# Program order of the input and attention stages bound by edges, and three kinds of small additions placed on GpSimd

## The chip, the cores and the metric

The kernel runs on one core of a Trainium2 chip. Its time is the time of one execution on the device in microseconds (us), and the number that counts is the median of the timed runs. A core has five engines that run side by side, each through its own queue and strictly in that queue's order: TensorE (PE, with its weight loads as PEld), VectorE (DVE), ScalarE (ACT), GpSimd (POOL) and SyncE (SP), which here only issues DMAs. An instruction whose input is not there holds up everything behind it on its engine.

## The reference

One decoder block on a sequence of 1024 tokens with 16 meta tokens ahead, width 1024, in float32. The part that this case turns on is the product with `w_in` (which gives the inputs of a convolution branch, q, k, v and two gates) and stick-breaking attention over 16 heads of 64:

```python
h = xn @ w_in
b_c, c_c, h_c, q, k, v, g_conv, g_attn = jnp.split(h, list(splits), axis=-1)
z = jnp.einsum("bqhd,bkhd->bhqk", qb, kb) * scale
log_beta = jax.nn.log_sigmoid(z)
log_fail = jnp.where(causal, log_beta - z, 0.0)
survive = lax.cumsum(log_fail, axis=3, reverse=True) - log_fail
a = jnp.where(causal, jnp.exp(log_beta + survive), 0.0)
o = jnp.einsum("bhqk,bkhd->bqhd", a, vb)
gate_attn = jax.nn.sigmoid(g_attn + b_gate[1])
merged = gate_conv * branch_conv + gate_attn * branch_attn
```

Behind it come the product with `w_out`, a norm, and a gated MLP with a short convolution. The change does not touch those.

## The kernel before, in words

Products in float32 are made of three matmuls on operands split in a high and a low part: high by high, high by low, low by high. The high part is a copy rounded by ACT, the low part a subtraction (source minus high) on DVE or POOL.

**Stages.** From 0 to about 560 us the input stage multiplies by `w_in` (partly in Strassen form) and writes q, k and v to DRAM as `qh_d`, `ql_d`, `kh_d`, `kl_d`, `vv_d`. From 560 to about 990 us runs attention. Behind it come the projections, the merge and the MLP, to 2028 us.

**Attention.** The work is cut in 8 pairs of heads, 2 heads each (`h`), 3 groups of query blocks each (`g`): 48 units. A group has three blocks of 114 queries. For each block:

- `scores` (lines 965 and 966): PE makes `z` of up to 512 keys at a time; it needs `qh`, `ql` and `kk`, which SP loads from DRAM for each head (`load_h`, six DMAs, lines 939 to 941) and `vv` once for a pair (`load_v`, lines 925 and 926).
- `fails` (line 971): ACT turns `z` into `fl` by a sigmoid.
- `scan` (line 982): one DVE instruction over all keys of the block, 128 to 1040 columns, in place in `fl`. It runs along the keys, so no part of `fl` is ready before the scan ends.

Then for each block of keys of the unit:

- `turn` (line 1001): PE transposes `fl` into `tp`.
- `high` and `lower` (lines 1006 and 447): ACT copies `tp` into `ah`, and DVE makes `al` = `tp` - `ah`. DVE alone does this.
- `weigh` (lines 1016 and 1017): PE adds `vv` by `ah`, then `vv` by `al`, to `av`.

A unit ends with three small steps: ACT copies one half of `av` into `half` (line 1039) and the other into `ot` (line 1042), and `out3` adds `half` to `ot` (line 1046). After the sixth unit of a pair `last_add` adds the column `ends` (line 1059), and SP stores `ot` (line 1062).

**Gates.** PE fills its time with the products of the gates: `plain` loads the raw weights of a gate (line 358), ACT makes `whi` (line 457), and two pieces of 512 columns make `wlo` (`lo_piece`, line 369). Then come 24 steps of three matmuls (lines 345 to 347), a sigmoid on ACT for each third (line 670), and a store of the gate (line 673). The first gate after the input stage is the bridge gate, still in the input stage; the twelve mid gates are made within attention. The weights of the first mid gate are prepared in the input stage already, so the first raw weights that attention loads are those of the second and third mid gate.

**What sets the order.** Each stage puts its steps into a `Plan`: engine, cost, key (a due time) and what has to be done before. `run` goes through a simulated time and always starts the ready step with the lowest key on each engine; the step's instructions are emitted at that moment. A step on `"ANY"` goes to whichever of DVE and POOL is free first in this simulation, and a `port` shared by POOL's work and the scans keeps the two apart in it. The emitted order is not the end of it: the framework has a scheduler of its own, which may put the instructions of an engine in another order as long as data dependences hold. `in_program_order` (at the end of the file) is meant to forbid this: it gives every instruction an edge to the one emitted before it on the same engine, over the range of instructions that two numbers mark. The range is taken from `first`, set ahead of the input stage's plan (line 440), and `last`, set behind attention's (line 1075). But `last` is assigned again in the last stage of the kernel (line 1671, `last = gi == len(groups) - 1`), so that the call at line 1718 gets `True`, and the range from `first` to 1 is empty: no edge is made.

Of the kernel before, what the change touches and what calls it, by code (L numbers as in the profile page):

```python
# [11 lines left out]
F32 = mybir.dt.float32  # L12
# [5 lines left out]
P = 128  # L18
# [5 lines left out]
NQ = NT - T0  # L24
CH = NQ // 3
# [89 lines left out]
def pe_cost(n):  # L115
    return (n / 2.4 + 13.0) / 1000.0


def act_cost(n):
    return 0.045 + 0.00091 * n  # L120


def dve_cost(n):
    return 0.07 + 0.00104 * n


def pool_cost(n):
    return 0.06 + 0.0023 * n


def any_cost(n):
    return {"DVE": dve_cost(n), "POOL": pool_cost(n)}
# [3 lines left out]
def block_kernel(ctx, tc, x, meta_tokens, g_pre_mix, w_in, channels, w_proj_conv,  # L136
                 w_proj_attn, w_out, g_post_mix, g_pre_ffn, w_up_gate, w_down,
                 g_post_ffn, out):
    nc = tc.nc

    def pool(name, bufs=1, side="left", space=None):
        kw = dict(name=name, bufs=bufs, reuse_waits="tile")
        if space is not None:
            kw["space"] = space
        else:
            kw["side"] = side
        return tc.tile_pool(**kw)
# [194 lines left out]
    def plain_step(ps, hi, lo, kb, a, n):  # L342
        k = slice(kb * P, (kb + 1) * P)
        xh, xl = src_x(kb, a, n)
        nc.tensor.matmul(ps, hi[:, k], xh, start=(kb == 0), stop=False)
        nc.tensor.matmul(ps, hi[:, k], xl, start=False, stop=False)
        nc.tensor.matmul(ps, lo[:, k], xh, start=False, stop=(kb == KB - 1))
# [8 lines left out]
    def load_raw(o):  # L356
        raw = wpool.tile([P, D], F32, name="raw", tag="raw")
        nc.sync.dma_start(raw, w_in[o])
        return raw

    def whole(raw):
        hi = wpool.tile([P, D], F32R, name="whi", tag="whi")
        lo = wpool.tile([P, D], F32R, name="wlo", tag="wlo")
        return hi, lo

    def lo_piece(raw, hi, lo, i, e="POOL", width=256):
        c = slice(width * i, width * i + width)
        eng = nc.vector if e == "DVE" else nc.gpsimd
        eng.tensor_tensor(lo[:, c], raw[:, c], hi[:, c].bitcast(F32), op=ALU.subtract)

    with ExitStack() as p0:
# [38 lines left out]
        for c in range(3):  # L410
            for b in range(3):
                x_block(3 * c + b)
                if c > 0 and b < 2:
                    if c == 1:
                        raw = first_raw[b]
                        hi, lo = whole(raw)
# [20 lines left out]
    tmp_e = sring.tile([P, 512], F32, name="tmp_e")  # L437
    snap_t = sring.tile([P, 2, 3, HS], F32, name="snap_e")

    first = len(nc.cur_bb.bb.instructions)  # L440
    plan = Plan({"raw": 2, "whi": 0, "wlo": 0, "ap": 4, "wk": 5, "st": 8, "xw": 2})

    def engine_of(e):
        return nc.vector if e == "DVE" else nc.gpsimd
# [1 line left out]
    def low(eng, out, src, hi):  # L446
        eng.tensor_tensor(out, src, hi.bitcast(F32), op=ALU.subtract)  # L447

    def plain(o, chunks, key, make, evac, finish, psum, first_chunk=0, given=None):
        st = {}  # L450
        if given is None:
            def load():
                st["raw"] = load_raw(o)

            def high():
                st["hi"], st["lo"] = whole(st["raw"])
                nc.scalar.copy(st["hi"], st["raw"])

            ld = plan.add("SP", 0.4, load, key=key - 16, takes=("raw",))
            h = plan.add("ACT", act_cost(D), high, (ld,), key - 10, ("whi", "wlo"))  # L460
            los = [plan.add("ANY", any_cost(512),
                            lambda e, i=i: lo_piece(st["raw"], st["hi"], st["lo"], i, e, 512), (h,),
                            key - 9 + 3 * i) for i in range(2)]
            plan.join(los, ("raw",))
        else:
            st["hi"], st["lo"], los = given
        before, evacs = None, []
        for ci in range(first_chunk, 3):
            a, n = chunks[ci]

            def step(kb, ci=ci, a=a, n=n):
                if kb == 0:
                    st["ps", ci] = psum()[:, :n]
                plain_step(st["ps", ci], st["hi"], st["lo"], kb, a, n)

            for kb in range(KB):
                at = key + (8 * (ci - first_chunk) + kb) * 3 * pe_cost(CH)
                before = plan.add("PE", 3 * pe_cost(n), lambda kb=kb, step=step: step(kb),
                                  (before, los[kb // 4] if los else None), at,
                                  (plan_bank,) if kb == 0 else ())  # L480

            def out(ci=ci, a=a, n=n):
                if ci == first_chunk and make is not None:
                    make()
                evac(a, n, st["ps", ci])

            evacs.append(plan.add("ACT", act_cost(n), out, (before,) + tuple(evacs[-1:]), at - 4,
                                  ("wk",) if ci == first_chunk and first_chunk == 0 else (),
                                  (plan_bank,)))
        plan.join((before,), ("whi", "wlo"))  # L490
        finish(evacs[-1:], at)
# [125 lines left out]
    for kb in range(4):  # L617
        st = {}
# [15 lines left out]
        key, t_step = 14.0 * kb, 3.0  # L634
# [3 lines left out]
        for j, (name, dst, x1, x2) in enumerate((("T1", "o1", "o1", "e1"), ("T2", "o1", "o2", "o1"),  # L638
# [12 lines left out]
            h = plan.add("ACT", act_cost(HT), high, (d,), k2)  # L651
# [8 lines left out]
    def late_tile(u):  # L660
        return lambda: u["t"]
# [37 lines left out]
    for i, name in enumerate((("v", 0), ("q", 0))):  # L699
        u = {"t": first_out[i]}  # L700
        o, k, done = block[name]
        plain(o, CH_K, at, None, lambda a, n, ps, u=u: nc.scalar.copy(u["t"][:, a:a + n], ps),
              lambda after, key, done=done, k=k, u=u: done(k, late_tile(u), after, key), bank,
              2, (*first_ops[i], None))
        at += item / 3
    for name in (("k", 0), ("v", 1), ("q", 1), ("k", 1)):
        o, k, done = block[name]
# [23 lines left out]
    def strassen_pair(i, at):  # L731
# [49 lines left out]
        evacs = [[], []]  # L781
        made = [None, None]
        b = {}
        last = {}

        def product(k, s, which, start, tok, hold):
            name = names[k]
# [44 lines left out]
        p = {}  # L832
# [43 lines left out]
    def next_high():  # L876
# [4 lines left out]
    h = plan.add("ACT", act_cost(D), next_high, (ld,), at - 10, ("whi", "wlo"))  # L881
# [9 lines left out]
    ps_mm = psA.enter_context(pool("ps_mm", 2, space=PSUM))  # L891
# [13 lines left out]
    plan = Plan({"raw": 2, "whi": 1, "wlo": 1, "mm": 2, "z": 2, "tp": 3, "av": 1, "qk": 3, "vv": 2,  # L905
                 "ot": 2, "wk": 2, "ah": 4, "al": 4, "half": 1, **{f"fl{b}": n for b, n in enumerate(FL)}})
# [12 lines left out]
    for p in range(NPAIR):  # L919
        ot_parts = []  # L920
# [9 lines left out]
        for h in range(2):  # L930
# [18 lines left out]
            for g in range(3):  # L949
# [38 lines left out]
                ust, readers, last_av = {}, {b: [] for b in scans}, av_last  # L988
# [44 lines left out]
                a0, b0 = (0, 64) if h == 0 else (64, 0)  # L1033
# [7 lines left out]
                def out2(g=g, p=p, a0=a0, ust=ust):  # L1041
                    nc.scalar.copy(out_tiles[p][a0:a0 + 64, CH * g:CH * (g + 1)], ust["av"][a0:a0 + 64])

                def out3(e, g=g, p=p, a0=a0, ust=ust):
                    o = out_tiles[p][a0:a0 + 64, CH * g:CH * (g + 1)]
                    engine_of(e).tensor_tensor(o, o, ust["half"][a0:a0 + 64], op=ALU.add)

                t_o = t_av + share[g] * half_pair
                o1 = plan.add("ACT", act_cost(CH), out1, (last_av,), t_o - 4,
                              ("half", "ot") if (h, g) == (0, 0) else ("half",))  # L1050
                o2 = plan.add("ACT", act_cost(CH), out2, (last_av, o1), t_o - 4, (), ())
                plan.join((o1, o2), ("av",))
                ot_parts.append(plan.add("ANY", any_cost(CH), out3, (o1, o2), t_o, (), ("half",)))
            plan.join(z_users, ("qk",))
        plan.join(v_users, ("vv",))

        def last_add(e, p=p):
            ov = out_tiles[p][:, :NQ].rearrange("p (b n) -> p b n", n=QB)
            engine_of(e).tensor_tensor(ov, ov, ends[:, p].unsqueeze(2).to_broadcast([P, 9, QB]), op=ALU.add)

        fin = plan.add("ANY", any_cost(NQ), last_add, tuple(ot_parts), t_o + 1)
        plan.add("SP", 0.4, lambda p=p: nc.sync.dma_start(o_d[p * P:(p + 1) * P, :], out_tiles[p][:, :NQ]),
                 (fin,), t_o + 1, (), ("ot",))

    for i, (which, ob) in enumerate(mid_gates):
        key = whole_time * i / len(mid_gates)
        outs = gate_out(which, ob, lambda: work.tile([P, NT], F32, name="gt", tag="wk", bufs=2), ("wk",))
        if i == 0:
            plain(0, CH_Q, key, *outs, lambda: ps_mm.tile([P, 512], F32, name="mm", tag="mm"), 0,
                  (nxt["hi"], nxt["lo"], None))  # L1070
        else:
            plain(48 + 8 * which + ob, CH_Q, key, *outs,
                  lambda: ps_mm.tile([P, 512], F32, name="mm", tag="mm"))
    plan.run()
    last = len(nc.cur_bb.bb.instructions)
    psA.close()

    work_ctx.close()
# [532 lines left out]
    for i in range(1, len(pairs)):  # L1611
        p, gate = divmod(i, 2)
# [57 lines left out]
    for gi, fbs in enumerate(groups):  # L1670
        last = gi == len(groups) - 1
# [13 lines left out]
        for tb in range(8):  # L1685
# [3 lines left out]
            for hf in range(2):  # L1689
# [13 lines left out]
                if last:  # L1703
                    sq = dw.tile([P, 512], F32, name="sq", tag="sq", bufs=2)
                    nc.scalar.activation(sq, a, AF.Square, accum_out=ssqs[tb][:, hf:hf + 1])
                    eng = nc.vector if (tb == 7 and hf) else nc.gpsimd
                    eng.tensor_tensor(a, a, g_post2[:, c], op=ALU.mult)
            next(prep, None)
            if last:
# [3 lines left out]
                for hf in range(2):  # L1713
# [1 line left out]
                    nc.vector.scalar_tensor_tensor(a[:, c], a[:, c], r, hb[:, c],  # L1715
                                                   op0=ALU.mult, op1=ALU.add)
                    (nc.sync if hf else nc.scalar).dma_start(out[tb * P:(tb + 1) * P, c], a[:, c])
    in_program_order(tc, nc, first, last)


def in_program_order(tc, nc, first, last):
    before = {}
    for ins in list(nc.cur_bb.bb.instructions)[first:last]:
        if ins.engine in before:
            tc.add_manual_dep(ins, before[ins.engine].name,
                              mybir.DependencyInfo(mybir.DependencyClass.NoSync,
                                                   mybir.DependencyReason.DATA),
                              reason="program order")
        before[ins.engine] = ins
# [57 lines left out]
```

## Time and profile before

| | us |
|---|---|
| median of 3 runs | 2033.87 |
| lowest and highest run | 2029.52 and 2034.86 |
| the profiled execution | 2030.09 |
| its span, first to last instruction | 2028.3 |

The page of the profiled execution gives these busy times over the whole span (share of it, instructions):

```profile
PE 1931.6 (95%) x12732; PEld 1811.0 (89%) x12732; DVE 1161.1 (57%) x1784; ACT 842.6 (42%) x1766; POOL 580.1 (29%) x432
```

Such a row is a mean over stages that differ. In a row of a stretch, further down, the numbers are start and end, length, then the busy us of PE, PEld, DVE, ACT and POOL with the number of instructions in brackets, the clock granted to TensorE (1.00 is full speed), the busy share of the DMA engines, and GB/s. In a row of a wait, the engine with its tile and line stands ahead of the arrow, and what it waited for behind it; then total us, how often, and the longest. In a row of the timeline the first two numbers are start and duration, and square brackets hold the idle time ahead of the instruction and what ended it.

### The profile page before, as it was taken

What the parts mean: (1) busy time and instruction counts of PE and PEld (TensorE: products, weight loads), DVE (VectorE), ACT (ScalarE), POOL (GpSimd) and SP (SyncE); (2) the same over time, 40 slices, a digit from 0 to 9 for tenths busy, and PEclk for the clock granted to TensorE, in tenths of its full rate; (3) what the DMA queues carried; (4) which work ended last, traced back from release to release, by engine and by line L of the source; (5) the groups of instructions that cost most, each with busy time, mean ns of one, the idle gap of its engine ahead of it and who ended that gap; (6) DMA issues with size and microseconds to landing.
All of it is one profiled execution on the core that took longest, in us unless ns stands there. A gap on an engine that the chain in (4) does not pass through costs nothing.

```text
span 2028.3 us, 32023 instructions
## 1 busy us (share of the span) xinstructions
PE 1931.6 (95%) x12732; PEld 1811.0 (89%) x12732; DVE 1161.1 (57%) x1784; ACT 842.6 (42%) x1766; POOL 580.1 (29%) x432
## 2 busy tenths in 40 slices
PE   6999999999988998989999999979999999999997
PEld 6999999999988888888899999968988998878886
DVE  6846666656368778787641116884354435345547
ACT  5533333444355566565541223453344344321122
POOL 1110000001101010010122560336555555654353
PEclk9999999999989999999999999989999999999999
DMA  3522222455684445441285673313221212253223
GB/s 137 161 84 74 83 64 64 145 143 166 181 187 127 118 128 128 113 117 58 84 271 148 188 211 124 105 32 118 70 84 63 104 63 84 75 182 117 84 84 135
DMA packets 73842, 238.56 MB, mean 118 GB/s; under 512 B 15400, under 2 KB 17224, under 8 KB 72668
## 3 DMA queue, kind: packets, MB, share of 16 engines
q1 hardware_dynamic: 70368, 226.00, 37.4%
q10 hardware_dynamic: 3324, 10.50, 1.6%
q8 instruction: 100, 1.64, 0.3%
q14 instruction: 50, 0.41, 0.1%
HBM read 166.02 MB, written 70.46 MB: 117 GB/s over the span
## 4 chain that ended last, share of the span: by engine, by line
PE 74%; DVE 13%; DMA 5%; ACT 3%; POOL 2%; issue 2%; SPq 0%; ACTq 0%; DVEq 0%; POOLq 0%
PE st L796 7%; PE st L799 7%; PE st L798 7%; PE st L1403 6%; PE st L1407 6%; PE st L1405 6%; DVE fl L982 5%; PE st L1697 3%; PE st L1695 3%; PE st L1696 3%; PE mm L245 2%; PE tp L1001 2%; PE mm L246 2%; PE mm L247 2%; DVE al L447 2%
## 5 line engine op out<-in xcount | busy, mean ns | idle before, releaser
L982 DVE TENSOR_TENSOR_SCAN fl<-fl,upper 114x128 f32<-114x128 f32 (+3 forms) x144 | 205.6, 1445 | 30.8 <-ACT fl L971 18.9
L173 POOL TENSOR_TENSOR a_op<-raw,a_op 128x512 fp32r<-128x512 f32 (+1 forms) x136 | 192.5, 1428 | 87.7 <-ACT a_op L172 85.5
L796 PE MATMUL st<-tT,s_op 128*128 128x260 f32 x672 | 190.9, 284 | 0.0
L799 PE MATMUL st<-tT,s_op 128*128 128x260 f32 x672 | 190.1, 283 | 0.0
L798 PE MATMUL st<-tT,s_op 128*128 128x260 f32 x672 | 190.0, 283 | 0.0
L1403 PE MATMUL st<-opT,a_op 128*128 128x258 f32 (+2 forms) x528 | 171.0, 324 | 5.2 <-ACT snap L1418 3.1
L1405 PE MATMUL st<-opT,a_op 128*128 128x258 f32 (+2 forms) x528 | 168.9, 320 | 2.6 <-DVE opT L173 1.7
L1407 PE MATMUL st<-opT,a_op 128*128 128x258 f32 (+2 forms) x528 | 168.7, 320 | 0.0
L1702 DVE TENSOR_TENSOR acc<-acc,st 128x512 f32<-128x512 f32 x144 | 98.4, 687 | 91.2 <-PE st L1697 91.2
L172 ACT CAST a_op<-raw 128x512 fp32r<-128x512 f32 (+1 forms) x136 | 85.1, 634 | 155.9 <-DMA raw<-in_w_up_gate_dram 52.7
L1006 ACT CAST ah<-tp 114x342 fp32r<-114x342 f32 (+3 forms) x288 | 105.8, 403 | 95.3 <-PE tp L1001 91.2
L447 DVE TENSOR_TENSOR al<-tp,ah 114x342 fp32r<-114x342 f32 (+3 forms) x288 | 118.0, 442 | 45.7 <-ACT ah L1006 44.1
L796 PE MATMUL st<-xnT,s_op 128*128 128x260 f32 x504 | 142.4, 283 | 0.0
L799 PE MATMUL st<-xnT,s_op 128*128 128x260 f32 x504 | 142.3, 282 | 0.0
L798 PE MATMUL st<-xnT,s_op 128*128 128x260 f32 x504 | 141.8, 281 | 0.0
L176 DVE TENSOR_TENSOR raw<-raw 128x512 f32<-128x512 f32 x72 | 73.8, 1026 | 108.1 <-POOL a_op L173 106.3
L751 ACT CAST s_op<-raw 128x512 fp32r<-128x512 f32 x126 | 78.2, 622 | 135.4 <-PE st L799 115.5
L447 DVE TENSOR_TENSOR s_op<-raw,s_op 128x512 fp32r<-128x512 f32 x121 | 84.4, 698 | 78.8 <-ACT s_op L751 78.3
L1017 PE MATMUL av<-al,vv 114*128 114x342 f32 (+3 forms) x288 | 92.1, 332 | 38.3 <-DVE al L447 37.5
L1405 PE MATMUL st<-opB,a_op 128*128 128x512 f32 (+2 forms) x396 | 127.4, 322 | 0.0
L1403 PE MATMUL st<-opB,a_op 128*128 128x512 f32 (+2 forms) x396 | 127.4, 322 | 0.0
L1407 PE MATMUL st<-opB,a_op 128*128 128x512 f32 (+2 forms) x396 | 126.9, 321 | 0.0
(224 smaller groups left out, 5880.4 us busy)
## 6 DMA issues: line engine op xcount, KB each, us to landing
raw<-in_w_in_dram SPq DMA_DIRECT2D x64, 512.0 KB
raw<-in_w_up_gate_dram SPq DMA_DIRECT2D x44, 512.0 KB
act_d<-owork SPq DMA_DIRECT2D x22, 512.0 KB
araw<-act_d SPq DMA_DIRECT2D x22, 512.0 KB
raw<-in_w_down_dram SPq DMA_DIRECT2D x22, 512.0 KB
qh<-qh_d SPq DMA_DIRECT2D x32, 256.5 KB
ql<-ql_d SPq DMA_DIRECT2D x32, 256.5 KB
vv_d<-vt SPq DMA_DIRECT2D x16, 512.0 KB
```

Source lines behind the costliest of these rows:

```text
L173: (lo_engine or nc.vector).tensor_tensor(lo, src, hi.bitcast(F32), op=ALU.subtract)
L447: eng.tensor_tensor(out, src, hi.bitcast(F32), op=ALU.subtract)
L796: nc.tensor.matmul(ps, wt[:, 0, c], xh, start=start and kb == 0, stop=False, skip_group_check=True)
L798: nc.tensor.matmul(ps, wt[:, 0, c], xl, start=False, stop=False, skip_group_check=True)
L799: nc.tensor.matmul(ps, wt[:, 1, c], xh, start=False, stop=kb == 3, skip_group_check=True)
L982: nc.vector.tensor_tensor_scan(fl[:, ::-1], fl[:, ::-1], upper[:, NT - nk:][:, ::-1], 1.0, op0=ALU.mult, op1=ALU.max)
L1006: nc.scalar.copy(kst["ah"][:n, off:], kst["tp"][:n, off:CH])
L1017: nc.tensor.matmul(av[:, off:], w, kst["al"][:n, off:], start=False, stop=(kb == nkb - 1))
L1403: nc.tensor.matmul(ps, wt[:, 0, k], xh, start=start and kb == 0, stop=False, skip_group_check=True)
L1405: nc.tensor.matmul(ps, wt[:, 0, k], xl, start=False, stop=False, skip_group_check=True)
L1407: nc.tensor.matmul(ps, wt[:, 1, k], xh, start=False, stop=stop and kb == 3, skip_group_check=True)
L1702: nc.vector.tensor_tensor(a, a, ps, op=ALU.add)
```

## The change

It has two parts.

First, the two marks get names of their own, `pin_from` and `pin_to`, which nothing assigns again. So the edges are made: in the input stage, in attention and in what lies between, every engine's instructions, SP's DMAs included, keep the order in which the plans emitted them.

Second, three kinds of steps of attention's plan go from `"ANY"` to `"POOL"`, with POOL's cost: `out3` (48 additions of 64x342), `last_add` (8 of 128x1026), and the `wlo` pieces of the mid gates that attention's plan itself prepares (11 gates, two pieces each of 128x512). The gates and products of the input stage keep `"ANY"`.

```diff
-    first = len(nc.cur_bb.bb.instructions)
+    pin_from = len(nc.cur_bb.bb.instructions)
...
-    def plain(o, chunks, key, make, evac, finish, psum, first_chunk=0, given=None):
+    def plain(o, chunks, key, make, evac, finish, psum, first_chunk=0, given=None, eng="ANY"):
...
-            los = [plan.add("ANY", any_cost(512),
-                            lambda e, i=i: lo_piece(st["raw"], st["hi"], st["lo"], i, e, 512), (h,),
+            los = [plan.add(eng, any_cost(512) if eng == "ANY" else pool_cost(512),
+                            lambda e="POOL", i=i: lo_piece(st["raw"], st["hi"], st["lo"], i, e, 512), (h,),
                             key - 9 + 3 * i) for i in range(2)]
...
-        last = {}
...
-                def out3(e, g=g, p=p, a0=a0, ust=ust):
+                def out3(e="POOL", g=g, p=p, a0=a0, ust=ust):
...
-                ot_parts.append(plan.add("ANY", any_cost(CH), out3, (o1, o2), t_o, (), ("half",)))
+                ot_parts.append(plan.add("POOL", pool_cost(CH), out3, (o1, o2), t_o, (), ("half",)))
...
-        def last_add(e, p=p):
+        def last_add(e="POOL", p=p):
...
-        fin = plan.add("ANY", any_cost(NQ), last_add, tuple(ot_parts), t_o + 1)
+        fin = plan.add("POOL", pool_cost(NQ), last_add, tuple(ot_parts), t_o + 1)
...
             plain(48 + 8 * which + ob, CH_Q, key, *outs,
-                  lambda: ps_mm.tile([P, 512], F32, name="mm", tag="mm"))
+                  lambda: ps_mm.tile([P, 512], F32, name="mm", tag="mm"), eng="POOL")
     plan.run()
-    last = len(nc.cur_bb.bb.instructions)
+    pin_to = len(nc.cur_bb.bb.instructions)
...
-    in_program_order(tc, nc, first, last)
+    in_program_order(tc, nc, pin_from, pin_to)
```

The names of lines behind 784 are one less after the change, since the line `last = {}` is gone (it was not used there).

What this does to the queues shows in the order of instructions. On DVE, in the unit that runs at 624 to 632 us before, these rows stood one after the other (L982 is a scan, named for its opcode; L447 makes `al`; L1046 is `out3`):

```order
L982 SCALAR_TENSOR_TENSOR fl_6960<-fl_6960,upper_6120 114x812
L1046 TENSOR_TENSOR ot_6385<-ot_6385,half_6981 64x342
L447 TENSOR_TENSOR al_7008<-tp_6977,ah_6993 128x342
L447 TENSOR_TENSOR al_7015<-tp_6986,ah_6998 114x228
L982 SCALAR_TENSOR_TENSOR fl_7006<-fl_7006,upper_6120 114x926
L447 TENSOR_TENSOR al_7024<-tp_7001,ah_7020 114x114
L447 TENSOR_TENSOR al_7044<-tp_7026,ah_7036 128x342
L1046 TENSOR_TENSOR ot_7041<-ot_7041,half_7042 64x342
L447 TENSOR_TENSOR al_7093<-tp_7032,ah_7056 114x342
L447 TENSOR_TENSOR al_7124<-tp_7051,ah_7070 114x342
```

At the same place on DVE after the change (numbers of buffers shift a little, L981 is the scan):

```order
L981 SCALAR_TENSOR_TENSOR fl_6963<-fl_6963,upper_6120 114x812
L447 TENSOR_TENSOR al_7006<-tp_6980,ah_6996 128x342
L447 TENSOR_TENSOR al_7013<-tp_6989,ah_7001 114x228
L447 TENSOR_TENSOR al_7027<-tp_7004,ah_7023 114x114
L447 TENSOR_TENSOR al_7047<-tp_7029,ah_7039 128x342
L981 SCALAR_TENSOR_TENSOR fl_7011<-fl_7011,upper_6120 114x926
L447 TENSOR_TENSOR al_7092<-tp_7035,ah_7058 114x342
L447 TENSOR_TENSOR al_7101<-tp_7053,ah_7073 114x342
```

The scan of 926 columns goes behind the `al` of 114x114 that ends the unit and behind the first `al` of the next one, and the two `ot` additions are gone to POOL.

On SP, at the change from the input stage to attention, the last stores of k, q and v and the first loads of heads stood so before (L358 is a raw weight of a mid gate, here the second's and the third's; L597 stores v, L552 and L554 store q and k; L939 begins the loads of the first head):

```order
L358 DMA raw<-in_w_in_dram 128x1024
L597 DMA vv_d<-vt 128x1024 x2
L597 DMA vv_d<-vt 114x256
L358 DMA raw<-in_w_in_dram 128x1024
L552 DMA qh_d<-hi 128x1026
L554 DMA ql_d<-su 128x1026
L552 DMA kh_d<-hi 128x1040
L554 DMA kl_d<-su 128x1040
L939 DMA qh<-qh_d 64x1026
```

After the change the stores of k are followed by the store of the bridge gate (L673), which stood five loads further back, and then by the loads of heads and of `vv` without a break:

```order
L554 DMA kl_d<-su 128x1040
L673 DMA ga_d<-gt 128x1026
L938 DMA qh<-qh_d 64x1026
L939 DMA kk<-kh_d 64x1040
L940 DMA ql<-ql_d 64x1026
```

The same queue of SP after the change, 18 loads of heads and one pair of `vv` loads further on:

```order
L939 DMA kk<-kl_d 64x1040
L940 DMA ql<-ql_d 64x1026
L924 DMA vv<-vv_d 128x2048
L925 DMA vv<-vv_d 114x256
L358 DMA raw<-in_w_in_dram 128x1024 x2
L673 DMA ga_d<-gt 128x1026
```

The two raw weights have moved from ahead of all loads of heads to behind those of three heads and of both `vv`. On ACT the cast of the first of them (L457) moved likewise, from ahead of the bridge gate's last sigmoid to behind the eight sigmoids of attention's first scores.

## The prediction

> **What bounds the kernel now.** I read the busy time by stretch first, with the granted clock beside it. Columns: stretch and its length, busy us (instructions) of PE, PEld, DVE, ACT and POOL, clock, DMA share, GB/s.
>
> ```profile
> 44.00:558.00 514.00, 513.95 (x4124) 513.55 (x4122) 308.96 (x469) 208.51 (x420) 46.21 (x36) 1.00 0.39 115
> 560.00:990.00 430.00, 384.95 (x2553) 358.78 (x2554) 333.43 (x469) 257.97 (x657) 47.76 (x32) 0.97 0.46 118
> ```
>
> The first row is the input stage, the second attention; the edges cover both. In the input stage PE is busy 513.95 of 514 us at full clock: an order that serves PE better has nothing to win there. In attention PE stands idle 430 - 384.95 = 45 us, and a clock of 0.97 costs 0.03 x 430 = 13 us more. Everything the change can win is in these 58 us. The view of waits over 550 to 1010 us says what PE waited for (total, times, longest).
>
> ```profile
> DVE al L447 <- ACT ah L1006: 44.1, 42, 2.7
> PE av L1017 <- DVE al L447: 37.5, 32, 2.6
> DVE ot L1046 <- ACT ot L1042: 25.2, 23, 2.6
> PE z L966 <- DMA ql<-ql_d: 4.1, 1, 4.1
> ACT half L1039 <- POOL ot L1046: 3.9, 3, 1.3
> ```
>
> 37.5 us of the 45 are one wait: the second matmul of a weigh step (`av`, line 1017) waits for DVE's `al`; another 4.1 are the first scores waiting for a load. No row has PE waiting for a scan. DVE is busy only 333 of 430 us, so it does not lack time; what stands ahead of the awaited `al` in DVE's queue decides. The timeline at 626 to 631 us, rows of DVE, POOL and PE (start, duration), and the clock around it:
>
> ```profile
> 626.42 0.51 DVE L1046 TENSOR_TENSOR ot<-ot,half 64x342 f32<-64x342 f32 x1
> 627.08 1.91 POOL L1059 TENSOR_TENSOR ot<-ot,ends 128x1026 f32<-128x1026 f32 x1 [19.67 <-DVE ot L1046]
> 627.70 3.23 DVE L982 TENSOR_TENSOR_SCAN fl<-fl,upper 114x926 f32<-114x926 f32 x1
> 630.85 0.67 DVE L447 TENSOR_TENSOR al<-tp,ah 114x114 fp32r<-114x114 f32 x2
> 631.15 0.32 PE L1017 MATMUL av<-al,vv 114*128 114x114 f32 x1 [2.58 <-DVE al L447]
> ...
> 628.55:631.15 2.60, 0.02 (x2) 0.00 (x1) 2.60 (x3) 0.43 (x1) 0.43 (x1) 1.00 0.82 324
> 631.97:635.38 3.41, 3.41 (x15) 3.33 (x14) 1.45 (x3) 1.86 (x6) 0.00 (x0) 0.50 0.00 0
> ```
>
> A scan of 926 columns stands ahead of a small `al`; PE idles 2.58 us for it and then runs 3.41 us at half clock, which costs 1.7 us more. The same shape comes back every pair of heads; the last long one is this.
>
> ```profile
> 959.49 0.34 PE L1017 MATMUL av<-al,vv 114*128 114x114 f32 x1 [2.51 <-DVE al L447]
> ```
>
> On the clock, the Trainium skill ("TensorE: Matmul & The Clock Gate", on why this matters for your kernels) puts the bound for a drop at idle gaps of about 3 us. By that rule gaps of this size would cost nothing beyond themselves and the win below would be about 6 us smaller. The rows above differ, 2.58 us was enough, and the measurement decides.
>
> **The change, part by part.**
>
> *Edges, attention, DVE.* In the order shown with the change, the scan of 926 goes behind the two `al` that it held up, and the `ot` addition leaves the queue. I followed the 32 waits of the `al` row in the same way: nearly all have, ahead of the `al`, a scan that goes behind the `al`, or an `ot` addition that leaves DVE. So what can be had is 37.5 us of gaps and, of the 13 us of clock, the part behind these gaps, some 9: 46 us. Not all of it comes. An `al` that no scan holds still needs ACT's `ah` (44.1 us of DVE waits in the list). I take 70%: **-32 us**; the bounds are 30% (-14) and 90% (-41).
>
> What is late next is the scan: put behind up to a few `al` of 0.50 us each (the row of groups below), it ends later for the transposes that read it. Before, PE never waited for one. The longest, 1040 columns, occurs 16 times; one `al` too many on each is 16 x 0.50 = 8 us, none is 0. I take **+4 us**, the middle, since neither end is nearer to a row.
>
> *Additions and low parts on GpSimd.* Groups of attention by form (times | busy us, mean ns):
>
> ```profile
> L1046 POOL TENSOR_TENSOR ot<-ot,half 64x342 f32<-64x342 f32 x4 | 7.0, 1738 | 37.6 <-ACT ot L1042 37.6
> L1046 DVE TENSOR_TENSOR ot<-ot,half 64x342 f32<-64x342 f32 x44 | 23.3, 531 | 25.6 <-ACT ot L1042 25.2
> L1059 DVE TENSOR_TENSOR ot<-ot,ends 128x1026 f32<-128x1026 f32 x4 | 4.9, 1221 | 0.0
> L447 DVE TENSOR_TENSOR al<-tp,ah 114x342 fp32r<-114x342 f32 x144 | 69.2, 501 | 30.0 <-ACT ah L1006 29.4
> L982 DVE TENSOR_TENSOR_SCAN fl<-fl,upper 114x926 f32<-114x926 f32 x16 | 37.6, 2352 | 2.5 <-ACT fl L971 2.5
> L982 DVE TENSOR_TENSOR_SCAN fl<-fl,upper 114x1040 f32<-114x1040 f32 x16 | 37.1, 2318 | 3.6 <-ACT fl L971 3.6
> ...
> 591.32 0.83 POOL L1046 TENSOR_TENSOR ot<-ot,half 64x342 f32<-64x342 f32 x1 [16.24 <-ACT ot L1042]
> ```
>
> DVE loses 23.3 + 4.9 = 28 us of work and the 25.2 us that it stood blocked behind ACT in front of an `ot` (part of what cures the gaps, so not counted again). POOL gains 44 additions of 0.83 (alone, last row) to 1.74 us (mean beside DVE's work) and four of 1.9: 44 to 84 us on an engine that is busy 48 of 430. That it is slower than DVE there shows on PE only through `half`, whose next writer is ACT: the 3.9 us row is that wait with only four additions on POOL. A unit of heads lasts about 9 us (430/48), so an addition of 1.7 us is done long before. Cost nothing there, at most 4.
>
> The price is on the scans. The 926 scans take 2352 ns, more than the 1040 ones at 2318; by width 926 is worth 2064, so those that lie beside POOL's work pay. The Trainium skill ("SBUF — State Buffer", on who interferes with whom) has the rule that an instruction of DVE with two SBUF inputs and one of GpSimd lock each other out, while an operand in PSUM leaves DVE free. It speaks against the change; the 3.23 us scan agrees with it, and `al`, which reads PSUM, keeps its 501 ns. From the rows: scans fill about half of attention, so half of 44 to 84 us, 22 to 42, can come back onto DVE against 28 taken off. DVE's busy time ends between -6 and +14. It has 97 us of slack, so I count 0, with +10 as the bad end.
>
> *Edges, first loads of attention (SP).* This is the loss. Before, SP issues the raw weights of the second and third mid gate at 528.53 and 534.95, ahead of all loads of heads. With the edges the same two stand behind the 18 loads of three half pairs and two of `vv` (order shown with the change). The timeline and DMA rows:
>
> ```profile
> 528.53 0.33 SPq L358 DMA_DIRECT2D raw<-in_w_in_dram  x1
> 534.95 0.34 SPq L358 DMA_DIRECT2D raw<-in_w_in_dram  x1
> 553.36 0.33 SPq L673 DMA_DIRECT2D ga_d<-gt  x1
> 562.38 0.45 PE L966 MATMUL z<-kk,ql 128*114 128x128 f32 x1 [4.14 <-DMA ql<-ql_d]
> 572.14 1.06 ACT L457 CAST whi<-raw 128x1024 fp32r<-128x1024 f32 x1 [0.76 <-issue]
> 573.32 0.41 PE L345 MATMUL mm<-xnT,whi 128*128 128x342 f32 x1
> ...
> ql<-ql_d SPq DMA_DIRECT2D x8, 256.5 KB
> kk<-kl_d SPq DMA_DIRECT2D x4, 260.0 KB
> vv<-vv_d SPq DMA_DIRECT2D x2, 1024.0 KB
> ga_d<-gt SPq DMA_DIRECT2D x2, 513.0 KB
> raw<-in_w_in_dram SPq DMA_DIRECT2D x2, 512.0 KB
> ...
> 552.50:587.50 35.00, 29.09 (x167) 27.68 (x166) 20.68 (x25) 15.23 (x37) 1.80 (x1) 0.86 1.04 226
> ```
>
> The store of the gate (line 673) now heads this row of loads; it waits for ACT's sigmoid, which comes about 1 us earlier since the cast of the raw weights no longer lies ahead of it: start at about 552.5. Ahead of and with the first raw then go 0.53 (store) + 18 x 0.264 + 2 x 1.05 and small remainders + 0.52 = about 8.1 MB. At 226 GB/s, the rate of this stretch with all DMA engines full (share 1.04), that is 36 us: it lands at 588.5. Then ACT's cast 1.06, POOL's first low part (1.80, the one piece in this row), and PE can go on at about 591, where it took up the second mid gate at 573.32 before. PE's order there is unchanged, and it is served strictly in order: nothing behind can step in. **+18 us.** ACT is stuck in its queue on the same cast, with the casts `ah` of the first unit behind a second such cast, so that the first `av` is late again by 1 to 2 us: +1.5. After so long a gap the clock falls; the longest such stretch in the trace is
>
> ```profile
> 1324.88:1335.12 10.24, 4.96 (x24) 4.99 (x25) 7.33 (x14) 6.62 (x9) 0.00 (x0) 0.50 0.16 49
> ```
>
> and costs half of its 4.96 us of PE work: +2.5. Together **+22 us**. Bounds: +13 (the loads served faster, no second delay) and +29 (twice the clock loss, the raw 4 us later).
>
> *Input stage.* ACT, DVE and SP change places a little while PE is full: 0, at most +2 if a load slips behind stores. *End of attention.* POOL instead of DVE for the last addition and the `ends`: 1.7 + 1.9 against 0.53 + 1.22, +1 us, of which gates hide most: +0.5. Everything after 990 us is the same.
>
> **Sum:** -32 + 4 + 0 + 22 + 0.5 = -5.5 us. The profiled execution took 2030.09 us (span 2028.3 of it): 2024.6. The three timed runs lie from 2029.52 to 2034.86 about 2033.87, so the profiled one is a fast one among them; I say **2025 us** for the median.
>
> **The rivals.**
>
> *Slower: lock-out of the scans.* Place: every unit's `ot` addition falls beside a scan, on the way to the `al` that PE waits for. Price: such a scan ends 1.2 us later, as the 926 did at 627.70 (3.23 against 2.06), and PE with it. Five hits (6 us) bring the sum above before, ten above it by more than a measurement can miss; 15 of the 48 additions give back 18 of the 32 us. Time: 2030 - 14 + 4 + 22 = **2042**. For it: the 926 row and the 3.23 us. Against: after the change few scans stand right ahead of an awaited `al`. Chance 0.25. The Trainium skill's rule on who interferes with whom would lead here, if it ruled in every third unit.
>
> *No change: the gain is paid back at the first gate.* The steady part wins about 22, as PE then waits for `ah` through `al`, and the late weights cost 22: **2031** with the small terms. For it: 44.1 us of `al` waiting for ACT. Chance 0.28.
>
> *Full gain.* The raw weights land by about 580 (a shorter queue than I add up) and nine tenths of the gaps go: 2030 - 41 + 8 = **1997**. Against: the DMA share of 1.04. Chance 0.09.
>
> *The edges bind nothing.* Then only the GpSimd part is left. The rows of SP and DVE do change places, so I give it nothing.
>
> **How the numbers follow.** The forecast has 0.38, with its own range of 2012 to 2029. A difference under 0.3% (6 us) cannot be told from none by measuring this kernel. Below 2028: the forecast nearly whole (0.36) and full gain (0.09), with a little of the rival at 2031 (0.02): 0.47. Above 2040: the lock-out nearly whole, 0.23, and 0.03 for a first gate at its bad end: 0.26. Between: 0.27. For 8 in 10, I leave out the better part of full gain and the worst of the lock-out: 2002 to 2047.
>
> **What would show each step.** The wait PE `av` <- DVE `al` should fall from 37.5 to about 12, with a new row of `tp` <- `fl` of some 4 us, and the clock in the steady part to rise to 0.99. DVE's row `ot` vanishes; POOL has 48 of 0.83 to 1.8 us. The mean of the scans of 926 shows the lock-out: above 2.6 us it rules. In the stretch 565 to 600 a single PE gap of about 18 us should wait for `whi` or `wlo`, behind a raw landing near 588. If that gap is under 8 us, the sum falls to near 2010; if `av` <- `al` stays above 25 us, the time is 2035 or more.

## The result and the profile after

| | before | after |
|---|---|---|
| median of 4 runs, us | 2034.22 | 2004.04 |
| lowest and highest | 2029.52 and 2034.86 | 1999.84 and 2005.19 |
| the profiled execution, us | 2030.09 | 2005.19 |

The ratio is 0.9853, with a 95% interval of 0.9832 to 0.9874. The kernel is 30 us faster by these medians, 24.9 by the two profiled executions. Runs of the kernel before beside the later experiments have medians of 2027 to 2031, so that 23 to 30 us is what can be said. The direction was forecast; the gain is about three times the 9 us that 2025 stood for.

To see where it comes from, I compared the end of each head's last `av` (the second matmul of `weigh`) in the two traces. PE has done the same number of matmuls by then in both (4501 at the end of the first head, later within 9), so that the times can be set against each other. After is ahead by 0.75 us in the input stage, behind by 16.2 us at the end of the first head, ahead by 28.7 at the end of attention, and by 25.0 at the end of the kernel. So attention first loses 17 us, then gains 45, and 4 are lost behind it.

**The loss.** The timeline of after at the start of attention (start, duration):

```profile
574.51 0.75 PE L1000 MATMUL tp<-ident,fl 114*128 114x114 f32 x6
576.48 1.63 SPq L358 DMA_DIRECT2D raw<-in_w_in_dram  x2
588.01 1.04 ACT L457 CAST whi<-raw 128x1024 fp32r<-128x1024 f32 x1 [14.96 <-DMA raw<-in_w_in_dram]
589.14 3.75 POOL L369 TENSOR_TENSOR wlo<-raw,whi 128x512 fp32r<-128x512 f32 x3 [47.90 <-ACT whi L457]
590.90 0.73 PE L964 MATMUL z<-kk,qh 128*114 128x464 f32 x1 [15.64 <-ACT fl L970]
```

This is the stall that was forecast: the raw weights were there at 588.0 (forecast 588.5), and PE went on at 590.9 (forecast 591). The gap is 15.6 us and not 18, since PE had work up to 575.3 where the forecast has it stop at 573.3. It is put down to a sigmoid `fl` and not to `whi`: these scores stand just ahead of the gate's product in PE's order, and their sigmoid stood on ACT behind the casts.

**The gain.** Waits of after, the first two from 590 to 970 us, the others from 550 to 990:

```profile
PE z L964 <- ACT fl L970: 16.5, 2, 15.6
PE av L1016 <- DVE al L447: 7.1, 12, 1.4
...
DVE al L447 <- ACT ah L1005: 77.6, 64, 16.9
PE z L964 <- DMA kk<-kl_d: 5.1, 1, 5.1
PEld tp L1000 <- DVE fl L981: 1.0, 3, 0.3
```

PE's wait for `al` fell from 37.5 to 7.1 us. DVE's own wait for ACT's `ah` rose from 44.1 to 77.6 (16.9 of it in the stall), and outside of the stall PE does not feel it. No scan makes PE's weight loads wait more than 0.3 us. From the end of the first head to the end of attention, before and then after:

```profile
599.30:998.62 399.32, 358.29 (x2398) 332.25 (x2397) 312.48 (x447) 242.10 (x617) 45.14 (x30) 0.98 0.40 106
615.54:969.91 354.37, 345.30 (x2398) 326.61 (x2398) 285.87 (x399) 238.00 (x617) 104.85 (x78) 1.00 0.44 119
```

For the same 2398 matmuls PE's idle time falls from 41 to 9 us, which makes 32 of the 45 us. The other 13 are busy time. The clock, 0.98 before and 1.00 after, accounts for about 8 of them (0.02 x 399); the remaining 5 are not explained. A stretch in the middle of attention, before (two pairs of heads) and then after (slightly more, two pairs take 96.8 us there):

```profile
729.70:839.40 109.70, 98.27 (x662) 91.87 (x661) 85.69 (x122) 65.85 (x168) 11.80 (x7) 0.98 0.46 119
```

```profile
715.00:813.00 98.00, 96.22 (x670) 91.58 (x670) 79.53 (x109) 65.02 (x169) 27.96 (x20) 1.00 0.50 133
560.00:970.00 410.00, 381.94 (x2614) 362.24 (x2615) 311.14 (x432) 259.31 (x670) 111.55 (x84) 0.97 0.48 127
```

PE idled 11.4 us of 109.7 and now 1.8 of 98, at full clock. The clock of the whole of attention still stands at 0.97 (second row), and that is the stall's doing: behind the first head it is 1.00, as shown above.

**DVE and GpSimd.** Groups of before:

```profile
L982 DVE TENSOR_TENSOR_SCAN fl<-fl,upper 114x128 f32<-114x128 f32 (+3 forms) x144 | 205.6, 1445 | 30.8 <-ACT fl L971 18.9
```

The same groups of after, then two forms of scans and POOL's additions:

```profile
L981 DVE TENSOR_TENSOR_SCAN fl<-fl,upper 114x470 f32<-114x470 f32 (+3 forms) x144 | 207.8, 1461 | 37.3 <-ACT fl L970 36.7
...
L981 DVE TENSOR_TENSOR_SCAN fl<-fl,upper 114x1040 f32<-114x1040 f32 x16 | 42.9, 2681 | 0.6 <-ACT fl L970 0.6
L981 DVE TENSOR_TENSOR_SCAN fl<-fl,upper 114x926 f32<-114x926 f32 x16 | 33.9, 2118 | 1.9 <-ACT fl L970 1.9
L1045 POOL TENSOR_TENSOR ot<-ot,half 64x342 f32<-64x342 f32 x48 | 59.8, 1246 | 211.1 <-ACT ot L1041 211.0
L1058 POOL TENSOR_TENSOR ot<-ot,ends 128x1026 f32<-128x1026 f32 x8 | 15.2, 1904 | 0.6
```

POOL's busy time in attention rises from 48 to 112 us, and all 144 scans together take 2.2 us more. That is not the price of POOL's work alone, since the scans stand in another order too; the section on e8 separates the two. Which scans are slow has changed: the 926 went from 2352 to 2118 ns, the 1040 from 2318 to 2681.

### The profile page after: what moved, and what is told of

The parts are those of the page before. It is cut to its first block, busy times and chain, and to the rows that moved or that the text cites. A ratio compares the mean times of both kernels' runs of the same rounds, so it can differ in the third digit from the quotient of the medians.

```text
span 2003.3 us, 32045 instructions
## 1 busy us (share of the span) xinstructions
PE 1922.9 (96%) x12732; PEld 1809.7 (90%) x12732; DVE 1129.5 (56%) x1730; ACT 838.2 (42%) x1766; POOL 646.9 (32%) x486
## 4 chain that ended last, share of the span: by engine, by line
PE 76%; DVE 10%; DMA 6%; ACT 3%; POOL 3%; issue 2%; SPq 0%; ACTq 0%; DVEq 0%; POOLq 0%
PE st L798 7%; PE st L795 7%; PE st L797 7%; PE st L1402 6%; PE st L1406 5%; PE st L1404 5%; DVE fl L981 3%; PE st L1696 3%; PE st L1694 3%; PE st L1695 3%; PE tp L1000 2%; PE mm L245 2%; PE mm L246 2%; PE mm L247 2%; PE mm L345 2%
## 5 line engine op out<-in xcount | busy, mean ns | idle before, releaser
L981 DVE TENSOR_TENSOR_SCAN fl<-fl,upper 114x470 f32<-114x470 f32 (+3 forms) x144 | 207.8, 1461 | 37.3 <-ACT fl L970 36.7
L447 DVE TENSOR_TENSOR al<-tp,ah 114x342 fp32r<-114x342 f32 (+3 forms) x288 | 116.4, 441 | 78.5 <-ACT ah L1005 77.6
L1045 POOL TENSOR_TENSOR ot<-ot,half 64x342 f32<-64x342 f32 x48 | 59.8, 1246 | 211.1 <-ACT ot L1041 211.0
L798 PEld LDWEIGHTS st<-tT,s_op 128*128 128x128 f32 x672 | 126.8, 189 | 0.0
```

Source lines behind the costliest of these rows:

```text
L798: nc.tensor.matmul(ps, wt[:, 1, c], xh, start=False, stop=kb == 3, skip_group_check=True)
L981: nc.vector.tensor_tensor_scan(fl[:, ::-1], fl[:, ::-1], upper[:, NT - nk:][:, ::-1], 1.0, op0=ALU.mult, op1=ALU.max)
```

## The experiments

My theory (A): the edges make the steady gain through DVE's order, SP's order costs some 17 to 22 us at the first gate, and the move to GpSimd does next to nothing. Times are medians; a ratio is to the kernel before beside them. In each fence of waits the columns are total us, times, longest.

| run | bound by edges | us | ratio (95% interval) |
|---|---|---|---|
| e1 | all, additions free | 2003.66 | 0.9877 (0.9851 to 0.9904) |
| e2 | none, additions on GpSimd | 2032.27 | 1.0011 (0.9996 to 1.0026) |
| e3 | all but SP | 1980.87 | 0.9764 (0.9739 to 0.9790) |
| e4 | all, weights due earlier | 1986.43 | 0.9794 (0.9767 to 0.9822) |
| e5 | DVE alone | 1985.45 | 0.9790 (0.9766 to 0.9815) |
| e6 | PE, ACT and POOL | 2037.10 | 1.0042 (1.0026 to 1.0058) |
| e7 | all but SP, scans due earlier | 1980.65 | 0.9771 (0.9749 to 0.9793) |
| e8 | all but SP, additions free | 1982.79 | 0.9775 (0.9753 to 0.9798) |
| e9 | all but SP, scans put ahead on DVE | 2033.93 | 1.0023 (1.0009 to 1.0036) |
| e10 | SP alone | 2044.59 | 1.0067 (1.0048 to 1.0086) |

### e1 and e2: one part each

e1 is the kernel before with the two marks renamed:

```diff
-    in_program_order(tc, nc, first, last)
+    in_program_order(tc, nc, pin_from, pin_to)
```

> Only the edges, the three kinds of additions stay free to go to DVE or GpSimd. Theory A (DVE's order makes the steady gain of 45 us, the change of SP's order costs 17 us at the first gate): 2004 to 2012 us, and PE's wait for al in the steady part falls to between 7 and 20 us. Rival B (taking the additions off DVE makes the steady gain): the loss at the first gate stays and little is gained, 2035 to 2050 us, the wait for al stays near 35 us.

e2 is the changed kernel without that call:

```diff
-    in_program_order(tc, nc, pin_from, pin_to)
```

> Only the additions and low parts on GpSimd, no edges. Theory A: 2022 to 2036 us, the wait for al stays above 25 us since the scans still stand ahead of it. Rival B: 1985 to 1995 us, the steady gain without the late weights.

The waits of PE in e1, at the first gate and for `al`:

```profile
PE mm L345 <- ACT whi L457: 13.9, 1, 13.9
PE av L1017 <- DVE al L447: 7.4, 12, 1.1
```

The wait of PE in e2:

```profile
PE av L1016 <- DVE al L447: 41.7, 36, 3.0
```

The edges alone give the whole result, stall and gain, and here PE's gap waits for `whi`. GpSimd alone gives no change: its interval takes in 1. Rival B falls. In the one trace of e2 this is the sum of two parts: e2 is 9.0 us ahead of before at the end of the first head and 0.8 at the end of attention.

### e3 and e4: the late weights

In e3 the loop that makes the edges passes over SP, so that SP's queue at the first gate is again that of before while all other engines keep the order of after:

```diff
     for ins in list(nc.cur_bb.bb.instructions)[first:last]:
+        if ins.engine == mybir.EngineType.SP:
+            continue
```

> The changed kernel with the edges on every engine but SP; SP then stands in the order of before, all other engines in that of after. Theory A: the PE gap of 15.6 us at the first gate goes, and with it 15 to 19 us of the time: 1985 to 1990 us. Rival C (the steady part takes up the lost time anyway, since the loads that come late there were early for the later heads): 1998 to 2005 us.

e4 keeps all edges and gives the loads of the first two raw weights a due time of their own:

```diff
-            ld = plan.add("SP", 0.4, load, key=key - 16, takes=("raw",))
+            ld = plan.add("SP", 0.4, load, key=key - 16 if due is None else due, takes=("raw",))
...
+                  due=-30.0 if i < 3 else None)
```

> The changed kernel with all edges; the two raw weights get a due time that puts them behind the first head's loads and the first vv, ahead of the second head's. Theory A: the first raw lands at about 572, ahead of its use at 575, and the time is 1986 to 1992 us. Rival C: 1998 to 2005 us. If the second head's loads, now 1 MB later, are what PE waits for next, a gap waiting for qh, kk or ql shows and the time is 1992 to 1998 us.

PE's waits in e3:

```profile
PE av L1016 <- DVE al L447: 8.1, 13, 1.4
PE z L965 <- DMA ql<-ql_d: 2.9, 1, 2.9
```

PE's waits in e4, and ACT's wait for the raw weights there:

```profile
PE av L1016 <- DVE al L447: 7.8, 12, 1.4
PE z L964 <- DMA kk<-kl_d: 5.1, 1, 5.1
...
568.83 1.04 ACT L457 CAST whi<-raw 128x1024 fp32r<-128x1024 f32 x1 [2.85 <-DMA raw<-in_w_in_dram]
```

The stall goes in both. e3 is 2004.04 - 1980.87 = 23 us faster than the change. In the two traces the instructions of PE, DVE, ACT and POOL stand in the same order throughout, and SP's differ in one stretch of 32 DMAs, where attention begins: 23 us is the price of SP's order there. Rival C, that the steady part takes it up, falls: after is 21.7 us behind e3 at the end of the first head and still 21.7 at the end of the last.

e4 lacks 5.6 us of that, although its weights arrive in time. Its loads of heads begin at 553 us, behind the store of the gate, as in after, where e3 issues the first of them at 543 and the weights at 528 and 535. PE waits 5.1 us for the first scores there, 2.9 in e3; the rest is open.

### e5 and e6: which engine's order

e5 makes the edges for DVE alone, e6 for PE, ACT and POOL (none for DVE and SP), both by such a condition in the loop:

```diff
     for ins in list(nc.cur_bb.bb.instructions)[first:last]:
+        if ins.engine != mybir.EngineType.DVE:
+            continue
```

> The changed kernel with edges on DVE alone; PE, ACT, POOL and SP stand as the framework's scheduler puts them. Theory A (DVE's order is the whole steady gain): 1979 to 1986 us, as with SP alone unbound. Rival D (PE's and ACT's orders have to fit DVE's): 1990 to 2010 us, with PE waiting for al or ah again.

> The changed kernel with edges on PE, ACT and POOL, none on DVE and SP. Theory A: 2020 to 2036 us, PE waits for al over 30 us as in the run with GpSimd alone. Rival D (the orders of the other engines carry part of the gain): 1995 to 2015 us.

PE's wait in e5:

```profile
PE av L1016 <- DVE al L447: 9.8, 13, 1.4
```

PE's wait in e6:

```profile
PE av L1016 <- DVE al L447: 42.9, 29, 3.8
```

DVE's order carries nearly all of the gain: bound alone it is within 5 us of e3, and with DVE free the other three gain nothing. e6 is the sharper of the two: in its trace PE, ACT and POOL stand exactly as in e3 and SP differs by one pair, so that 2037.10 - 1980.87 = 56 us are DVE's order alone. e5 says less of PE, since the scheduler puts PE's instructions nearly as the plan does (49 of 12732 places differ from e3). So rival D falls for the edges, which are worth 5 us at most on the other engines; that PE's order does not matter is not shown, and e9 below comes back to it.

### e7 and e9: what it is in DVE's order

Both pass over SP as e3 does. e7 changes the due time of the scans:

```diff
-                    scans[b] = plan.add("DVE", dve_cost(2 * nk), scan, tuple(sigs), t_b + 1, port=True)
+                    scans[b] = plan.add("DVE", dve_cost(2 * nk), scan, tuple(sigs), t_b - 3, port=True)
```

> SP unbound, all else bound; the scans' due time is 4 us earlier, which puts one to three more scans ahead of 134 of the 288 al than in the run with SP unbound (before has more ahead of 114). Theory A (a scan ahead of an awaited al makes the gap): PE's wait for al rises from 8 us to 25 to 45 us and the time from 1981 to 2000 to 2030 us. Rival E (being bound to the plan matters, not which scan stands where): 1979 to 1988 us.

The wait in e7:

```profile
PE av L1016 <- DVE al L447: 6.3, 9, 1.2
```

My theory missed here. One to three more scans stand ahead of 134 `al`, about as many as before the change, and nothing is lost. The order of the matmuls suggests why: with the scans due earlier the plan emits `al` later, and it puts the products that use it later as well, with steps of a gate in between. Between the last transpose of a block and its second product PE has 18.4 instructions on average (at least 8) in e7, 16.5 (at least 6) in e3. So I changed the theory: it is not the scan ahead of an `al` that costs, but one that stands there while PE's order still asks for the `al` at its old place (A2). e9 makes just that. PE, ACT and POOL have the orders of e3 without a difference, and on DVE each scan is taken past the `al` before it wherever the uses of that `al` were emitted later than the scan (and no circle of waits comes of it):

```diff
+    for i in sorted(scans):
+        j = dve.index(i)
+        for _ in range(3):
+            n = als.get(dve[j - 1])
+            if n is None or used[n] < i or (n + 3 < len(turns) and turns[n + 3] < i):
+                break
+            dve[j - 1], dve[j] = dve[j], dve[j - 1]
+            j -= 1
```

> As the run with SP unbound, with PE's, ACT's and POOL's orders exactly the same; on DVE alone each scan is put ahead of the al just before it wherever that can be done without a cycle, which puts a scan ahead of 96 more of the 288 al. Theory A2 (what costs time is a scan ahead of an al while PE's order still has that al's use at the old place; with the earlier due time the plan moved both): before has 170 such places in 114 al and lost 45 us by them, so 96 lose about 25 us: 1995 to 2015 us, and PE's wait for al is 20 to 40 us. Rival E (the place of the scans does not matter): 1979 to 1988 us.

The wait in e9, and PE's stretch from 720 to 820 us there:

```profile
PE av L1023 <- DVE al L447: 43.6, 55, 2.1
...
720.00:820.00 100.00, 88.68 (x588) 81.52 (x587) 71.75 (x101) 57.49 (x149) 23.15 (x17) 0.98 0.43 116
```

The whole gain is gone, by 78 of the 144 scans put ahead of one or two `al` each, 96 `al` in all, with the other engines' orders unchanged. Rival E falls, and the direction of A2 is borne out. The size is twice what I expected (53 us against 25), and why is not shown. A count of places leaves out that a scan which is moved ahead can wait for its own sigmoid, with the `al` behind it: DVE stands idle 56.2 us in front of scans in e9, 30.9 in e3 and 30.8 in the kernel before.

### e8: GpSimd once the order is right

e1's code with SP passed over as in e3.

> Only the edges, and SP unbound; the additions and low parts may go to DVE or GpSimd as before. Theory A: within 4 us of the run with SP unbound, 1977 to 1985 us. Rival F (GpSimd's additions are worth something once DVE's order is right, or the lock-out of the scans costs something): outside of that, either way.

PE's wait in e8:

```profile
PE av L1017 <- DVE al L447: 7.8, 13, 1.1
```

1982.79 against 1980.87 in e3, with intervals that overlap, and 2003.66 in e1 against 2004.04 after the change: no worth of the additions' place can be seen in the time, in either kernel.

The same pairs show what POOL's work costs the scans. All 144 of them take, in e1, e2, e8 and e3:

```profile
L982 DVE TENSOR_TENSOR_SCAN fl<-fl,upper 114x128 f32<-114x128 f32 (+2 forms) x144 | 202.2, 1420 | 33.5 <-ACT fl L971 32.3
L981 DVE TENSOR_TENSOR_SCAN fl<-fl,upper 114x128 f32<-114x128 f32 (+3 forms) x144 | 215.2, 1507 | 52.5 <-ACT fl L970 52.0
L982 DVE TENSOR_TENSOR_SCAN fl<-fl,upper 114x128 f32<-114x128 f32 (+2 forms) x144 | 201.2, 1414 | 27.7 <-ACT fl L971 26.8
L981 DVE TENSOR_TENSOR_SCAN fl<-fl,upper 114x470 f32<-114x470 f32 (+3 forms) x144 | 210.0, 1478 | 30.9 <-ACT fl L970 28.7
```

With the additions and low parts on POOL they take 5.6 us more with all edges (202.2 to 207.8), 8.8 with SP free (201.2 to 210.0), and 9.6 with no edge (205.6 before to 215.2). Within a pair the scans' order still differs a little, so these are estimates.

### e10: SP's order alone

```diff
     for ins in list(nc.cur_bb.bb.instructions)[first:last]:
+        if ins.engine != mybir.EngineType.SP:
+            continue
```

> The changed kernel with edges on SP alone: the late raw weights without the steady gain. Theory A (the late weights cost what the profile shows at the first gate, whatever comes behind): 2046 to 2056 us. Rival G (behind a stall the unbound steady part, with its 11 us of PE gaps for every two pairs, catches up): 2030 to 2042 us.

The waits of PE in e10 from 545 to 1030 us, and from its timeline the first cast of raw weights in attention:

```profile
PE av L1016 <- DVE al L447: 42.3, 40, 2.9
PE z L964 <- DMA kk<-kl_d: 3.2, 1, 3.2
PE mm L347 <- POOL wlo L369: 1.6, 1, 1.6
...
597.87 1.06 ACT L457 CAST whi<-raw 128x1024 fp32r<-128x1024 f32 x1
```

Between both expectations: 12 us over e2, where 23 was the price with all engines bound. The long stall is missing: the framework's scheduler has put attention's steps ahead of the gate's in PE's order (51 matmuls of the gate fewer lie before the end of the first head), and ACT casts the first weights at 597.87 us only. The other engines moved with SP, so this run does not give the price of SP's order by itself. What is lost is not caught up, though, against rival G: e10 is 13.2 us behind e2 at the end of the second head, where both have done the same number of matmuls, and 15.0 at the end of the last.

e3 and e7 are the fastest of all, 1981 us, and beat both kernels.

## Why the prediction was right in its direction and wrong in size

- **Input stage, 0:** after is 0.75 us ahead at its end. Right.
- **First loads, +22:** e3 against the change gives 23 us, 21.7 of them at the end of the first head. Place, mechanism and sum were right, the parts less so. The gap was 15.6 us and not 18, and PE starts on the first scores some 3 us later than in e3, since the loads of the first head stand behind the gate's store; the forecast saw that order and gave it no price. Against before, the first head ends only 16.2 us late, as e3 is 5.5 us ahead of before there. This lead is not the edges' doing, for e2 without any edge has 9.0: before, PE waits 4.1 us for the first scores and then runs at a clock of 0.50 (562.38 to 567.12 us), where e3 waits 2.9 and stays at 1.00.
- **DVE's order, -32:** this is the term that failed; it came out at -45, beyond its own bound of -41. I had 46 us to be had and took 70%, because an `al` that no scan holds would still wait for ACT's `ah`. The 45 us from the first head to the end of attention are nearly all of the 46, in after and in e3 alike (from 5.5 to 50.4 us ahead). That wait did grow, from 44.1 to 77.6 us, and PE did not wait for it: in PE's order a product stands far enough behind its transposes (16.5 instructions on average, as counted for e7). A wait of DVE was taken for a wait of PE. That it lands so near 46 is in part luck: the idle time gave 32 and not 37.5, the clock about 8 as I had it (9), and 5 have no term in the forecast.
- **Scans late, +4:** 0 by the profile (the longest wait for one is 0.3 us). The half of an unknown between 0 and 8 was too much.
- **GpSimd, 0:** right; neither e2 nor e8 shows a change in the time. POOL's work cost all scans together 5.6 to 9.6 us where I allowed 22 to 42 onto DVE, and the mean of the 926 stayed at 2.12 us, under the 2.6 that was to show the lock-out. The rival at 2042 falls with it.
- **End of attention, +0.5:** after loses 3.7 us behind attention (28.7 to 25.0 ahead). PE waits there as long as before (3.1 us after, 3.0 before, for `yT`, whose loads of `y_d` come at another time against the gates). What differs is the clock. The first row is a wait of after; the next is the stretch behind it, then the stretch behind the like wait of before (2.13 us long), and the last is a second slow stretch of after:

```profile
999.01 0.94 PE L245 MATMUL mm<-yT,whi 128*128 128x342 f32 x2 [2.34 <-ACT yT L172]
999.01:1002.73 3.72, 3.72 (x12) 3.40 (x13) 1.91 (x3) 0.70 (x2) 0.69 (x1) 0.50 1.02 212
1024.98:1031.81 6.83, 5.70 (x33) 5.14 (x34) 4.00 (x8) 1.95 (x5) 0.52 (x1) 1.00 0.92 306
1173.39:1176.80 3.41, 3.41 (x14) 3.41 (x14) 0.51 (x1) 0.62 (x1) 2.76 (x4) 0.50 0.87 306
```

At half the clock 3.72 us of work cost 1.9 us and 3.41 us cost 1.7, together nearly the whole. 3.7 us is also less than single executions of the kernel before differ by (2029.52 to 2034.86), and why the clock fell after one wait and not after the other is open.

With -45 for the steady part, +17 for the first head (22 less the lead of 5.5), 0 for the scans and +4 behind attention, the sum is -45 + 17 + 4 - 1 = -25, which is what the two profiles show. The step itself, that nearly every gap has ahead of its `al` a scan that the edges move behind, was right: by the two traces it holds for 26 of the 32 waits, 32.8 of 37.4 us, and e9 shows it from the other side; that the place of a scan alone decides was too simple, as e7 shows.

## What to carry to other kernels

When an order is written out by hand, look whether it is really in force: here an assigned name made it empty, and the scheduler left PE nearly in the plan's order (67 of 12732 places differ between e2 and e3) while DVE's no longer fitted it. A wait in front of an engine counts only as far as another engine's order asks for the result soon; judge a reordering by the pair of maker and user, not by what stands ahead in one queue. Binding an order binds its flaws too: the plan's own order of loads cost half of what its order of DVE won (23 of 45 us), and freeing that one queue got it back.

## What the runs showed of the hardware that was not expected

In these runs DVE and GpSimd did not pay alike for working side by side. The scans lost 5.6 to 9.6 us in all, as shown for e8. Of the 48 additions in the trace of after, the 31 that overlap a scan took 1.45 us on average and the 17 others 0.87, which makes 31 x 0.58 = 18 us for the additions. 27 of them began while a scan ran, and each of these ended 0.58 to 0.73 us after that scan (or the one right behind it), however early it had begun. One such pair:

```profile
740.98 2.08 DVE L981 TENSOR_TENSOR_SCAN fl<-fl,upper 114x926 f32<-114x926 f32 x1
741.53 2.26 POOL L1045 TENSOR_TENSOR ot<-ot,half 64x342 f32<-64x342 f32 x1 [0.67 <-ACT ot L1041]
```

The length of a gap alone does not tell whether the clock falls behind it. In the kernel before, PE stood idle 2.51 us from 739.82 us on and kept the clock of 1.00, while an idle time of 1.91 us was followed by half the clock:

```profile
739.82:742.33 2.51, 0.00 (x0) 0.00 (x1) 2.51 (x3) 0.41 (x1) 0.34 (x1) 1.00 0.80 323
742.33:746.00 3.67, 3.67 (x27) 3.62 (x28) 2.27 (x5) 2.89 (x8) 0.00 (x0) 1.00 0.03 12
697.76:699.67 1.91, 0.00 (x1) 0.00 (x1) 1.91 (x4) 0.06 (x1) 0.00 (x0) 1.00 0.49 165
700.24:703.65 3.41, 3.41 (x16) 3.36 (x15) 2.08 (x5) 1.79 (x5) 0.00 (x0) 0.50 0.00 1
```

So the forecast's "2.58 us was enough" holds for that gap and is no bound.
